# One block of a hybrid mLSTM decoder on Trainium2: the turned keys taken from the score products

## The chip, the cores and the metric

The kernel runs on one core of one Trainium2 chip. The metric is the device time of one execution in microseconds (us). The kernel before takes 1497.92 us, the median of three runs (1495.53 to 1499.62).

## What is computed

The program is one decoder block over 1024 positions of width 1024 in float32: a projection into 6664 columns, an mLSTM with 4 heads of 256 features beside a pooling branch, gates that merge the two, an output projection, and a gated feed-forward part. The change lies in the mLSTM. Cut to what matters, the reference computes for each head and each chunk of positions:

```
s = jnp.einsum('bhld,bhsd->bhls', qc, kc) * dexp          # scores, causal
num = w_inter[..., None] * jnp.einsum('bhvk,bhlk->bhlv', c_state, qc) + jnp.einsum('bhls,bhsv->bhlv', s, vc)
c_state = decay[..., None, None] * c_state + jnp.einsum('bhsv,bhsk->bhvk', vc * w[..., None], kc)
```

`dexp` is zero where the key's position `s` is later than the query's position `l`. The scores contract over the features of a key, the state over its positions, so the keys are needed in two orientations.

## The kernel before

Every float32 operand of a large product is split into two parts, a high part rounded to the engine's reduced float32 (`F32R`) and the rest (`split`, L131 and L132: a cast on ScalarE, a subtraction on VectorE). A product is then three matmuls, high by high, high by low and low by high (`mm3`, L143 to L145). The operands are written feature-major, 128 features on the partitions.

The mLSTM stage works on 16 items, 4 heads by 4 chunks of 256 positions (`items`, `c` is the chunk, `NC` is 4). For each item:

- `prepare` loads the keys `raw` (feature-major, two halves of 128 features), splits them into `k`, loads the two parts of the queries into `q`, the values into `v`, a row of gate numbers into `u`. Except in a head's last chunk it calls `turned`: four transposes on TensorE (L573, 128 by 128 each) put the keys position-major into one PSUM bank with the tag `aux`, and for each block of 128 positions ScalarE (L577) and VectorE (L578) scale them and split them into `kt`.
- `scores` makes the products of keys and queries, 12 matmuls of 256 columns into one bank: for both blocks `i` of 128 key positions and both feature halves `dk`, against all 256 query positions. Then it builds the decay factors in `dt`, multiplies them with the scores (L625) and splits the result into `ph` and `pl`. For the second block of keys only the second 128 query positions are read from the bank (`slice(384, 512)`).
- `update` makes the next state from `kt` and `v` (12 matmuls of 258 columns) and splits it into `cs`.
- `attend` makes the outputs from `cs` and `q`, from `v` and `ph`/`pl`, normalises them, turns them back (L683) and stores them into `ya`.

`second_branch` (L155, 24 matmuls of 512 columns a call) is put between the items as further work for TensorE; `project` makes its products. The loop runs over the items: it prepares item n+2, updates the state with item n, makes the scores of item n+1, then attends item n. The order in which each engine issues its instructions is not that of the code: a scheduler places them by its own forecast of times, and each engine then works in that order, waiting on semaphores. There are six PSUM banks with the tag `mm` and two with the tag `aux`; a bank is reused once all its readers are done.

Of the kernel before, what the change touches and what calls it, by code (L numbers as in the profile page):

```python
# [8 lines left out]
F32 = mybir.dt.float32  # L9
# [57 lines left out]
def tile_hybrid_block(ctx, tc, x, xt, consts, params, w_fm, w_v, w_pool, w_a, w_b, w_out, w_gate, w_up, w_down, out):  # L67
# [54 lines left out]
    def bank(tag="mm"):  # L122
        return psp.tile([P, 512], F32, tag=tag, name=tag, bufs=BANKS[tag])
# [429 lines left out]
    with ExitStack() as c4:  # L553
        t1 = pool(c4, "t1", 1)
        rc = pool(c4, "rc", 6)
        kp_ = pool(c4, "kp", 3)
        qp = pool(c4, "qp", 3)
        pp = pool(c4, "pp", 4)
        t2 = pool(c4, "t2", 2)
        vp = pool(c4, "vp", 3)  # L560
        ktp = pool(c4, "ktp", 3)

        def chunk(base, h, c):
            t = rc.tile([P, 2, 256], F32, tag="rc", name="rc")
            nc.sync.dma_start(out=t, in_=z_d[base + 2 * h:base + 2 * h + 2, :, c * 256:(c + 1) * 256].rearrange("i p n -> p i n"))
            return t

        def turned(dst, raw, scales):

            ps = bank("aux")  # L570
            for i in range(2):
                for f in range(2):
                    nc.tensor.transpose(out=ps[:, i * 256 + f * P:i * 256 + (f + 1) * P], in_=raw[:, f, i * P:(i + 1) * P], identity=ident)  # L573
            for i in range(2):
                src = ps[:, i * 256:(i + 1) * 256]
                hi, lo = dst[:, 0, i, 0:DH], dst[:, 1, i, 0:DH]
                nc.scalar.activation(out=hi, in_=src, func=AF.Copy, scale=scales[i])  # L577
                nc.vector.scalar_tensor_tensor(out=lo, in0=src, scalar=scales[i], in1=hi.bitcast(F32), op0=ALU.mult, op1=ALU.subtract)  # L578

        def prepare(h, c):  # L580
            it = {}
            raw = chunk(Z_K, h, c)
            k = it["k"] = kp_.tile([P, 2, 2, 256], F32R, tag="k", name="k")
            split(k[:, 0], k[:, 1], raw)
            it["made"] = split.last
            q = it["q"] = qp.tile([P, 2, 2, 256], F32R, tag="q", name="q")
            for a in range(2):
                src = q_d[a, 2 * h:2 * h + 2, :, c * 256:(c + 1) * 256]
                nc.sync.dma_start(out=q[:, a].bitcast(F32), in_=src.rearrange("i p n -> p i n"))
            u = it["u"] = t1.tile([P, 256], F32, tag="u", name="u", bufs=3)  # L590
            nc.sync.dma_start(out=u, in_=r_d[h, c * 256:(c + 1) * 256].partition_broadcast(P))
            v = it["v"] = vp.tile([P, 2, 2, VW], F32R, tag="v", name="v")
            nc.vector.tensor_copy(out=v[:, :, :, DH:VW], in_=norm[:, :, 2 * c:2 * c + 2, :])
            for a in range(2):
                src = v_d[a, c * 256:(c + 1) * 256, h * DH:(h + 1) * DH]
                it["loaded"] = nc.sync.dma_start(out=v[:, a, :, 0:DH].bitcast(F32), in_=src.rearrange("(i p) n -> p i n", p=P))
            if c < NC - 1:
                kt = it["kt"] = ktp.tile([P, 2, 2, DH], F32R, tag="kt", name="kt")
                turned(kt, raw, [e_put[:, 2 * c + i, h:h + 1] for i in range(2)])
            return it  # L600

        def scores(h, c, it):

            k, q, u = it["k"], it["q"], it["u"]
            ps = bank()
            for i in range(2):
                for dk in range(2):
                    l = [k[:, a, dk, i * P:(i + 1) * P] for a in range(2)]
                    r = [q[:, a, dk, :] for a in range(2)]
                    mm3(ps[:, i * 256:(i + 1) * 256], l, r, dk == 0, dk == 1)  # L610
            dt = t2.tile([P, 512], F32, tag="dt", name="dt")
            ph = pp.tile([P, 512], F32R, tag="p", name="ph")
            pl = pp.tile([P, 512], F32R, tag="p", name="pl")
            for i, jj in ((0, 0), (1, 1), (0, 1)):
                o = dt[:, i * 256 + jj * P:i * 256 + (jj + 1) * P]
                uu, b = u[:, jj * P:(jj + 1) * P], cd[:, jj - i, 2 * c + i, h:h + 1]
                if i < jj:
                    nc.scalar.activation(out=o, in_=uu, func=AF.Exp, bias=b, scale=-1.0)
                else:

                    nc.vector.tensor_scalar(out=o, in0=uu, scalar1=b, scalar2=0.0, op0=ALU.subtract, op1=ALU.max)
                    nc.scalar.activation(out=o, in_=o, func=AF.Exp, scale=-1.0)
                    nc.gpsimd.affine_select(out=o, in_=o, pattern=[[1, P]], compare_op=ALU.is_ge, fill=0.0, base=0, channel_multiplier=-1)
            for i, sl in enumerate((slice(0, 256), slice(384, 512))):
                nc.vector.scalar_tensor_tensor(out=dt[:, sl], in0=ps[:, sl], scalar=rsk[:, 2 * c + i:2 * c + i + 1], in1=dt[:, sl], op0=ALU.mult, op1=ALU.mult)  # L625
                split(ph[:, sl], pl[:, sl], dt[:, sl])
            it["p"] = ph, pl

# [16 lines left out]
        def attend(h, c, it, state):  # L645
            ss = t2.tile([P, 2], F32, tag="ss", name="ss")
            rd = t2.tile([P, 2], F32, tag="rd", name="rd")
            q, v, pr = it["q"], it["v"], it["p"]
            nums = []
            for jj in range(2):  # L650
                cl = 2 * c + jj
                num = t2.tile([P, VW], F32, tag="num", name="num", bufs=4)
                if c > 0:
                    ps = bank()
                    for dk in range(2):
                        mm3(ps[:, :VW], [q[:, a, dk, jj * P:(jj + 1) * P] for a in range(2)], [state[1][:, a, dk, :] for a in range(2)], dk == 0, dk == 1)
                    nc.scalar.activation(out=num, in_=ps[:, :VW], func=AF.Copy, scale=e_get[:, cl, h:h + 1])
                ps = bank()
                for i in range(jj + 1):
                    o = i * 256 + jj * P  # L660
                    mm3(ps[:, :VW], [a[:, o:o + P] for a in pr], [v[:, a, i, :] for a in range(2)], i == 0, i == jj)
                if c > 0:
                    nc.vector.tensor_add(out=num, in0=ps[:, :VW], in1=num)
                else:
                    nc.scalar.copy(out=num, in_=ps[:, :VW])
                r, den = rd[:, jj:jj + 1], num[:, DH:DH + 1]
                nc.vector.tensor_scalar(out=r, in0=den, scalar1=-1.0, scalar2=enm[:, cl, h:h + 1], op0=ALU.mult, op1=ALU.max)
                nc.vector.tensor_max(out=r, in0=den, in1=r)
                nc.vector.reciprocal(out=r, in_=r)

                nc.scalar.activation(out=rsb[:, jj * DH:(jj + 1) * DH], in_=num[:, :DH], func=AF.Square, scale=r, accum_out=ss[:, jj:jj + 1])
                nums.append(num)
            ms = t2.tile([P, 2], F32, tag="ms", name="ms")
            nc.vector.tensor_scalar(out=ms, in0=ss, scalar1=1.0 / DH, scalar2=EPS, op0=ALU.mult, op1=ALU.add)
            rs = t2.tile([P, 2], F32, tag="rs", name="rs")
            nc.gpsimd.tensor_tensor(out=rs, in0=ms, in1=nhalf[:, 0:2], op=ALU.pow)
            nc.vector.tensor_mul(out=rs, in0=rs, in1=rd)
            tr = bank("aux")
            for jj in range(2):
                hf = t2.tile([P, DH], F32, tag="hf", name="hf")  # L680
                nc.scalar.activation(out=hf, in_=nums[jj][:, :DH], func=AF.Copy, scale=rs[:, jj:jj + 1])
                for f in range(2):
                    nc.tensor.transpose(out=tr[:, f * 256 + jj * P:f * 256 + (jj + 1) * P], in_=hf[:, f * P:(f + 1) * P], identity=ident)  # L683
            sl = slice(c * 256, (c + 1) * 256)
            o = chunk(Z_O, h, c)
            for f in range(2):
                nc.vector.scalar_tensor_tensor(
                    out=o[:, f, :], in0=tr[:, f * 256:(f + 1) * 256], scalar=col(A_MH, 2 * h + f), in1=o[:, f, :], op0=ALU.mult, op1=ALU.mult)
            if h < H - 1:
                split(*(t[:, :, sl] for t in yat[h]), o)  # L690
                return
            for f in range(2):
                split(*(a[f][:, sl] for a in ya[h]), o[:, f, :])
# [33 lines left out]
        for n, (h, c) in enumerate(items):  # L727
            prepare_item(n + 2)
            if c == 0:
# [2 lines left out]
                    ya.append([[t[:, f, :] for f in range(2)] for t in yat[h]])  # L732
                else:
                    ya.append([[keep.tile([P, WIDE], F32R, tag="x", name="ya")[:, :S] for _ in range(2)] for _ in range(2)])
            nxt = update(h, c, its[n], state) if c < NC - 1 else None
            if n + 1 < len(items):
                scores(*items[n + 1], its[n + 1])
            attend(h, c, its[n], state)
            state = nxt
            for _ in range(YB[n]):  # L740
# [415 lines left out]
```

## Time and profile before

| | |
|---|---|
| median of three runs | 1497.92 us (1495.53 to 1499.62) |
| the profiled execution | 1498.39 us, its span 1496.7 us |
| TensorE (PE) busy | 1475.3 us, 99% of the span, 7067 matmuls |
| VectorE (DVE) busy | 1122.8 us, 75% |
| ScalarE (ACT) busy | 725.6 us, 48% |
| mean granted clock of TensorE | 0.996 of full speed |

A row of the profile gives the engine, the line of the kernel, the operation, and the names of what is written and read (`mm<-q,k` is a matmul into a bank `mm` with `q` moving and `k` as the weights). The duration of a matmul in such a row is the time from its start to its end, and matmuls overlap: a row of 392 ns says nothing of how close the next one follows. That is read from the starts in the timeline. PEld is the loading of weights, which overlaps the matmuls.

### The profile page before, as it was taken

How to read it: one execution, taken by the hardware profiler on the slowest of the kernel's cores; microseconds unless marked ns; L12 is line 12 of the kernel's file. 1: busy time of each engine (PE TensorE's matmuls, PEld its weight loads, DVE VectorE, ACT ScalarE, POOL GpSimd, SP SyncE). 2: the span in 40 equal slices, each digit the busy share in tenths (PEclk: the TensorE clock that was granted, in tenths of full speed). 3: DMA queues.
4: the chain of work that ended last, by engine and by line, in shares of the span. 5: the costliest groups of instructions: out<-in, count | busy, mean ns of one | idle time of the engine just before them, and what ended most of it. 6: DMA issues, size and time to landing. Idle time of an engine off the chain costs nothing.

```text
span 1496.7 us, 19610 instructions
## 1 busy us (share of the span) xinstructions
PE 1475.3 (99%) x7067; PEld 1245.3 (83%) x7067; DVE 1122.8 (75%) x2028; ACT 725.6 (48%) x1329; POOL 45.4 (3%) x74
## 2 busy tenths in 40 slices
PE   9999999999999999999999999999999999999997
PEld 9998888878887789997888778888888887888886
DVE  5757878797876678765557779888888885658945
ACT  6475655556553468772233455444444443332322
POOL 0000000000000011210000000000000000000022
PEclk9999999999999999999999999999999999999998
DMA  6662433243433498837534325443444435979653
GB/s 212 197 247 86 154 125 128 99 142 113 141 106 120 159 313 283 255 103 253 183 99 141 99 85 186 166 159 138 169 155 141 160 119 195 356 280 379 240 190 133
DMA packets 102448, 262.18 MB, mean 175 GB/s; under 512 B 9932, under 2 KB 47948, under 8 KB 102352
## 3 DMA queue, kind: packets, MB, share of 16 engines
q1 hardware_dynamic: 86608, 220.57, 42.6%
q10 hardware_dynamic: 15744, 40.38, 7.2%
q8 instruction: 55, 0.90, 0.2%
q14 instruction: 41, 0.34, 0.1%
HBM read 172.29 MB, written 88.62 MB: 174 GB/s over the span
## 4 chain that ended last, share of the span: by engine, by line
PE 94%; DMA 3%; DVE 2%; issue 1%; ACT 0%; SPq 0%; POOLq 0%; POOL 0%; DVEq 0%; ACTq 0%
PE mm L143 25%; PE mm L145 25%; PE mm L144 25%; PE mm L155 13%; PE aux L143 1%; PE aux L144 1%; PE aux L145 1%; DMA v<-v_d 1%; DMA tg<-tg_d 0%; DMA raw<-in_w_up 0%; PE mm L524 0%; DMA x<-in_xt 0%; PE aux L683 0%; DMA yb<-yb_d 0%; DMA rc<-z_d 0%
## 5 line engine op out<-in xcount | busy, mean ns | idle before, releaser
L131 ACT CAST s<-raw 128x512 fp32r<-128x512 f32 x220 | 133.6, 621 | 200.6 <-PE mm L145 164.1
L132 DVE TENSOR_TENSOR s<-raw,s 128x512 fp32r<-128x512 f32 x220 | 148.5, 687 | 30.1 <-ACT s L131 29.1
L143 PE MATMUL mm<-fd,s 128*128 128x512 f32 x352 | 137.7, 392 | 5.1 <-DVE e L234 2.7
L143 PE MATMUL mm<-zd,s 128*128 128x512 f32 x352 | 137.4, 393 | 0.3 <-DVE o L234 0.3
L144 PE MATMUL mm<-fd,s 128*128 128x512 f32 x352 | 137.7, 391 | 0.0
L145 PE MATMUL mm<-fd,s 128*128 128x512 f32 x352 | 137.5, 391 | 0.0
L145 PE MATMUL mm<-zd,s 128*128 128x512 f32 x352 | 137.3, 390 | 0.0
L144 PE MATMUL mm<-zd,s 128*128 128x512 f32 x352 | 137.1, 389 | 0.0
L143 PE MATMUL mm<-zb,s 128*128 128x512 f32 x264 | 103.9, 394 | 0.0
L144 PE MATMUL mm<-zb,s 128*128 128x512 f32 x264 | 102.8, 389 | 0.0
L145 PE MATMUL mm<-zb,s 128*128 128x512 f32 x264 | 102.7, 390 | 0.0
L144 PE MATMUL mm<-fb,s 128*128 128x512 f32 x264 | 102.7, 389 | 0.0
L143 PE MATMUL mm<-fb,s 128*128 128x512 f32 x264 | 102.7, 389 | 0.0
L145 PE MATMUL mm<-fb,s 128*128 128x512 f32 x264 | 102.7, 389 | 0.0
L144 PE MATMUL mm<-tg,a 128*128 128x512 f32 (+1 forms) x266 | 100.2, 377 | 0.0
L145 PE MATMUL mm<-tg,a 128*128 128x512 f32 (+1 forms) x266 | 100.0, 377 | 0.0
L143 PE MATMUL mm<-tg,a 128*128 128x512 f32 (+1 forms) x266 | 100.0, 377 | 0.0
L143 PEld LDWEIGHTS mm<-fd,s 128*128 128x128 f32 x352 | 66.4, 189 | 20.4 <-DVE e L234 3.2
L145 PEld LDWEIGHTS mm<-fd,s 128*128 128x128 f32 x352 | 66.5, 189 | 14.3 <-DVE s L132 0.4
L143 PEld LDWEIGHTS mm<-zd,s 128*128 128x128 f32 x352 | 66.1, 188 | 14.8 <-DVE o L234 0.8
L144 PEld LDWEIGHTS mm<-zd,s 128*128 128x128 f32 x352 | 66.1, 188 | 14.1 <-issue 0.5
L144 PEld LDWEIGHTS mm<-fd,s 128*128 128x128 f32 x352 | 66.4, 189 | 13.7
(345 smaller groups left out, 3508.5 us busy)
## 6 DMA issues: line engine op xcount, KB each, us to landing
tg_d<-t SPq DMA_DIRECT2D x77, 512.0 KB, 3.1
tg<-tg_d SPq DMA_DIRECT2D x77, 512.0 KB, 6.1
raw<-in_w_fm SPq DMA_DIRECT2D x44, 512.0 KB, 3.9
z_d<-o ACTq DMA_DIRECT2D x24, 512.0 KB, 2.9
raw<-in_w_gate SPq DMA_DIRECT2D x22, 512.0 KB, 3.7
raw<-in_w_up SPq DMA_DIRECT2D x22, 512.0 KB, 5.1
q_d<-x ACTq DMA_DIRECT2D x16, 512.0 KB, 2.7
rc<-z_d SPq DMA_DIRECT2D x32, 256.0 KB, 5.0
```

Source lines behind the costliest of these rows:

```text
L131: hi_made = cast(out=hi, in_=src)
L132: split.last = hi_made.ins, nc.vector.tensor_sub(out=lo, in0=src, in1=hi.bitcast(F32)).ins
L143: nc.tensor.matmul(out, lhsT=l[0], rhs=r[0], start=start, stop=False, skip_group_check=resume)
L144: nc.tensor.matmul(out, lhsT=l[0], rhs=r[1], start=False, stop=False, skip_group_check=resume)
L145: mm3.last = nc.tensor.matmul(out, lhsT=l[1], rhs=r[0], start=False, stop=stop, skip_group_check=resume)
L155: nc.tensor.matmul(ps[half], lhsT=l[a], rhs=r[half][b], start=(k == 0 and (a, b) == (0, 0)), stop=(k == nk - 1 and a == 1),)
```

## The change

`turned` no longer has transposes. Three standing tiles `q0`, `q1`, `q2` (printed below with the scheduler's numbers, as `q_4430`, `q_4431`, `q_4432`) take the place of the pool `q`: each holds the identity, the two feature halves of the queries' high part, the identity again, and the low part's halves. In `scores`, for all chunks but a head's last, the matmuls with high queries run over the queries and the identity beside them, so that the same weights give the scores and the keys turned, in one bank. For the first block of keys that makes, for each feature half, 384, 256 and 384 columns; for the second block, whose scores are now made for the second 128 query positions alone, 256, 128 and 256. The two blocks go to two banks, the first `mm`, the second `aux`. In a head's last chunk the second block's six matmuls shrink from 256 to 128 columns. `kt` has two buffers where it had three, and the loop makes the scores of item n+1 ahead of the update with item n.

```
-            ps = bank("aux")
-            for i in range(2):
-                for f in range(2):
-                    nc.tensor.transpose(out=ps[:, i * 256 + f * P:i * 256 + (f + 1) * P], in_=raw[:, f, i * P:(i + 1) * P], identity=ident)
...
-        ktp = pool(c4, "ktp", 3)
+        ktp = pool(c4, "ktp", 2)
...
+        qs = [t1.tile([P, 5 * 256], F32R, name=f"q{n}") for n in range(3)]
+        for t in qs:
+            for o in (0, 5 * P):
+                nc.vector.tensor_copy(out=t[:, o:o + P], in_=ident)
+
+        def blocks(t):
+            return t.rearrange("p (a n) -> p a n", n=P)
+
+        def turned(dst, src, scale):
+
+            hi, lo = (blocks(dst[:, a]) for a in range(2))
+            nc.scalar.activation(out=hi, in_=src, func=AF.Copy, scale=scale)
+            nc.vector.scalar_tensor_tensor(out=lo, in0=src, scalar=scale, in1=hi.bitcast(F32), op0=ALU.mult, op1=ALU.subtract)
...
-            q = it["q"] = qp.tile([P, 2, 2, 256], F32R, tag="q", name="q")
+            qt = it["qt"] = qs[len(its) % len(qs)]
+            q = it["q"] = [qt[:, o:o + 512].rearrange("p (i n) -> p i n", i=2) for o in (P, 6 * P)]
...
-            ps = bank()
-            for i in range(2):
-                for dk in range(2):
-                    l = [k[:, a, dk, i * P:(i + 1) * P] for a in range(2)]
-                    r = [q[:, a, dk, :] for a in range(2)]
-                    mm3(ps[:, i * 256:(i + 1) * 256], l, r, dk == 0, dk == 1)
+                s = []
+                for i in range(2):
+
+                    n = (2 - i) * P
+                    ps = bank("aux" if i else "mm")[:, :n + 2 * P]
+                    b = blocks(ps)
+                    for dk in range(2):
+                        l = [k[:, a, dk, i * P:(i + 1) * P] for a in range(2)]
+                        part = b[:, dk:dk + 3 - i]
+                        wide = blocks(it["qt"][:, dk * 3 * P:(dk + 1) * 3 * P])
+                        if i:
+                            wide = wide[:, 1:3] if dk else wide[:, 0:3:2]
+                        nc.tensor.matmul(part, lhsT=l[0], rhs=wide, start=dk == 0, stop=False, skip_group_check=True)
+                        nc.tensor.matmul(ps[:, P:P + n], lhsT=l[0], rhs=q[1][:, dk, i * P:], start=False, stop=False, skip_group_check=True)
+                        nc.tensor.matmul(part, lhsT=l[1], rhs=wide, start=False, stop=dk == 1, skip_group_check=True)
+                    turned(kt[:, :, i], b[:, 0::3 - i], e_put[:, 2 * c + i, h:h + 1])
+                    s.append(ps[:, P:P + n])
+            else:
+                ps = bank()
+                for i in range(2):
+                    for dk in range(2):
+                        l = [k[:, a, dk, i * P:(i + 1) * P] for a in range(2)]
+                        mm3(ps[:, i * 256 + i * P:(i + 1) * 256], l, [q[a][:, dk, i * P:] for a in range(2)], dk == 0, dk == 1)
+                s = [ps[:, 0:256], ps[:, 384:512]]
...
-                nc.vector.scalar_tensor_tensor(out=dt[:, sl], in0=ps[:, sl], scalar=rsk[:, 2 * c + i:2 * c + i + 1], in1=dt[:, sl], op0=ALU.mult, op1=ALU.mult)
+                nc.vector.scalar_tensor_tensor(out=dt[:, sl], in0=s[i], scalar=rsk[:, 2 * c + i:2 * c + i + 1], in1=dt[:, sl], op0=ALU.mult, op1=ALU.mult)
...
-            nxt = update(h, c, its[n], state) if c < NC - 1 else None
             if n + 1 < len(items):
                 scores(*items[n + 1], its[n + 1])
+            nxt = update(h, c, its[n], state) if c < NC - 1 else None
```

Three places of the order matter below. The first is TensorE's order where the projections (`zd`, `s`) end and the mLSTM stage begins. Before:

```order
L145 MATMUL mm<-zd_140,s 128x512
L573 MATMUL aux<-cst,rc 128x128 [waits DMAHW5_49,PE_49]
L573 MATMUL aux<-cst,rc 128x128 x3
L143 MATMUL mm<-q,k 128x256 [waits DMAHW6_49,Activation_49]
L155 MATMUL mm<-yb,wbh 128x512 x4
L155 MATMUL mm<-yb,wbl 128x512 [waits DVE_49]
```

And now:

```order
L145 MATMUL mm<-zd_140,s 128x512
L619 MATMUL mm<-q_4430,k 128x384 [waits DMAHW6_49,DVE_49,Activation_49]
L619 MATMUL aux<-q_4430,k 128x256 [waits PE_49]
L155 MATMUL mm<-yb,wbh 128x512 x4
L155 MATMUL mm<-yb,wbl 128x512 [waits DVE_49]
```

The four transposes are gone from ahead of the first call of `second_branch`, and two wide score matmuls stand where one of 256 columns stood; the wait for VectorE at `wbl` remains.

The second place is VectorE's order at the same time, where `wbl` is made. Before:

```order
L466 TENSOR_TENSOR o<-o,rsb 128x512 [waits DVE_49]
L593 COPY v<-norm 128x4x2 x2
L468 TENSOR_TENSOR o<-mm,rsb 128x512 [waits PE_49]
L593 COPY v<-norm 128x4x2
L132 TENSOR_TENSOR wbl<-raw,wbh 128x1024 [waits DMAHW1_49,Activation_49]
```

And now:

```order
L466 TENSOR_TENSOR o<-o,rsb 128x512 [waits DVE_49]
L571 CAST q_4430<-cst 128x128 x2
L571 CAST q_4431<-cst 128x128 x2
L571 CAST q_4432<-cst 128x128 x2
L596 COPY v<-norm 128x4x2
L596 COPY v<-norm 128x4x2 [waits PE_49]
L468 TENSOR_TENSOR o<-mm,rsb 128x512 [waits PE_49]
L596 COPY v<-norm 128x4x2
L132 TENSOR_TENSOR wbl<-raw,wbh 128x1024 [waits DMAHW1_49,Activation_49]
```

Six copies of the identity have come in ahead of `L468`, which waits for TensorE.

The third place is VectorE's order for the first two items. Before:

```order
L621 TENSOR_SCALAR dt<-u,cd 128x128
L578 SCALAR_TENSOR_TENSOR kt<-aux,e_put,kt 128x256 [waits Activation_49] x2
L132 TENSOR_TENSOR k<-rc,k 128x512 [waits DMAHW3_49,Activation_49]
L621 TENSOR_SCALAR dt<-u,cd 128x128 [waits DMAHW7_49]
L621 TENSOR_SCALAR dt<-u,cd 128x128
L625 SCALAR_TENSOR_TENSOR dt<-mm,rsk,dt 128x256 [waits PE_49,Pool_49]
L625 SCALAR_TENSOR_TENSOR dt<-mm,rsk,dt 128x128 [waits Pool_49]
```

And now:

```order
L132 TENSOR_TENSOR k<-rc,k 128x512 [waits DMAHW3_49,Activation_49]
L641 TENSOR_SCALAR dt<-u,cd 128x128 [waits DMAHW7_49]
L641 TENSOR_SCALAR dt<-u,cd 128x128
L580 SCALAR_TENSOR_TENSOR kt<-mm,e_put,kt 128x256 [waits Activation_49]
L645 SCALAR_TENSOR_TENSOR dt<-mm,rsk,dt 128x256 [waits Pool_49]
L580 SCALAR_TENSOR_TENSOR kt<-aux,e_put,kt 128x256 [waits Activation_49]
L645 SCALAR_TENSOR_TENSOR dt<-aux,rsk,dt 128x128 [waits Pool_49]
L580 SCALAR_TENSOR_TENSOR kt<-mm,e_put,kt 128x256 [waits Activation_49]
L645 SCALAR_TENSOR_TENSOR dt<-mm,rsk,dt 128x256 [waits Pool_49]
L132 TENSOR_TENSOR pl<-dt,ph 128x256 [waits Activation_49]
L580 SCALAR_TENSOR_TENSOR kt<-aux,e_put,kt 128x256 [waits Activation_49]
```

The making of the first item's `kt` has moved from ahead of its scores to behind them, among the scalings of the scores of the first and the second item.

## Rows read from the trace of the kernel before

**Rows 1.** The page: busy time of the engines, and the chain that ended last by engine.
```profile
PE 1475.3 (99%) x7067; PEld 1245.3 (83%) x7067; DVE 1122.8 (75%) x2028; ACT 725.6 (48%) x1329; POOL 45.4 (3%) x74
...
PE 94%; DMA 3%; DVE 2%; issue 1%; ACT 0%; SPq 0%; POOLq 0%; POOL 0%; DVEq 0%; ACTq 0%
```
**Rows 2.** Busy time by stretch; columns: us, PE, PEld, DVE, ACT, POOL, clock, DMA share, GB/s.
```profile
528.00:545.00 17.00, 16.15 (x101) 14.25 (x101) 12.65 (x30) 12.01 (x27) 1.08 (x4) 1.00 0.83 275
545.00:560.00 15.00, 15.00 (x106) 14.06 (x105) 12.50 (x46) 12.58 (x35) 3.06 (x8) 1.00 1.07 372
560.00:600.00 40.00, 40.00 (x290) 37.79 (x289) 34.74 (x127) 33.47 (x97) 6.21 (x14) 1.00 0.89 288
600.00:640.00 40.00, 39.94 (x263) 36.27 (x262) 29.29 (x106) 30.90 (x88) 8.41 (x16) 1.00 0.79 251
640.00:662.00 22.00, 22.00 (x176) 21.51 (x175) 18.39 (x61) 17.35 (x47) 2.70 (x5) 1.00 0.41 133
```
**Rows 3.** Timeline of PE, columns: start us, duration us, what; 512, 344 and 256 columns.
```profile
526.04 0.39 PE L143 MATMUL mm<-zd,s 128*128 128x512 f32 x1
...
526.95 0.39 PE L144 MATMUL mm<-zd,s 128*128 128x512 f32 x1
...
8.31 0.32 PE L144 MATMUL mm<-wv,zb 128*128 128x344 f32 x1
...
9.41 0.32 PE L145 MATMUL mm<-wv,zb 128*128 128x344 f32 x1
...
577.00 0.28 PE L144 MATMUL mm<-q,k 128*128 128x256 f32 x1
...
578.19 0.28 PE L145 MATMUL mm<-q,k 128*128 128x256 f32 x1
```
**Rows 4.** The chain that ended last, in order of time: four transposes of the keys.
```profile
545.11 0.44 PE aux L573 x4
```
**Rows 5.** Timeline of PE: products of one column, and plain float32 ones of 512 columns.
```profile
1463.33 1.62 PE L999 MATMUL aux<-cst,sq 128*128 128x1 f32 x14
1464.81 0.48 PE L143 MATMUL mm<-tg,a 128*128 128x512 f32 x1
...
507.05 1.88 PE L524 MATMUL mm<-x,raw 128*128 128x512 f32 x4
508.37 0.79 PE L143 MATMUL mm<-zb,s 128*128 128x512 f32 x1
```
**Rows 6.** The chain that ended last: four of those plain float32 matmul records.
```profile
507.21 1.72 PE mm L524 x4
```
**Rows 7.** Timeline of VectorE, and one row of PE, where the stage begins.
```profile
530.01 0.24 DVE L593 CAST v<-norm 128x8 fp32r<-128x8 f32 x2
531.41 0.69 DVE L468 TENSOR_TENSOR o<-mm,rsb 128x512 f32<-128x512 f32 x1 [1.16 <-PE mm L145]
...
532.09 2.35 DVE L132 TENSOR_TENSOR wbl<-raw,wbh 128x1024 fp32r<-128x1024 f32 x2
...
533.36 0.50 PE L155 MATMUL mm<-yb,wbl 128*128 128x512 f32 x1 [0.52 <-DVE wbl L132]
```
**Rows 8.** Groups by line and shape, 525 to 690 us: count, then busy us, mean ns.
```profile
L578 DVE SCALAR_TENSOR_TENSOR kt<-aux,e_put,kt 128x256 fp32r<-128x256 f32 x24 | 11.5, 477 | 1.1 <-ACT kt L577 1.0
L577 ACT ACTIVATE kt<-aux,e_put 128x256 fp32r<-128x256 f32 x24 | 11.3, 471 | 1.4 <-PE aux L573 1.3
...
L621 DVE TENSOR_SCALAR dt<-u,cd 128x128 f32<-128x128 f32 x32 | 7.8, 282 | 0.0
L625 DVE SCALAR_TENSOR_TENSOR dt<-mm,rsk,dt 128x256 f32<-128x256 f32 x16 | 7.7, 479 | 3.6 <-PE mm L145 3.6
```
**Rows 9.** Timeline of PE: its waits where the feed-forward part begins.
```profile
857.07 0.50 PE L143 MATMUL mm<-fd,s 128*128 128x512 f32 x1 [1.29 <-ACT s L131]
860.57 0.50 PE L143 MATMUL mm<-fd,s 128*128 128x512 f32 x1 [1.12 <-ACT e L230]
869.25 0.50 PE L143 MATMUL mm<-fd,s 128*128 128x512 f32 x1 [1.95 <-DVE e L234]
```

More of the change, by code (lines that the diff above doesn't have):

```diff
@@ L556, in tile_hybrid_block @@
         kp_ = pool(c4, "kp", 3)
-        qp = pool(c4, "qp", 3)
         pp = pool(c4, "pp", 4)
@@ L566, in chunk @@
             return t
-        def turned(dst, raw, scales):
-            ps = bank("aux")
-            for i in range(2):
-                for f in range(2):
-                    nc.tensor.transpose(out=ps[:, i * 256 + f * P:i * 256 + (f + 1) * P], in_=raw[:, f, i * P:(i + 1) * P], identity=ident)
-            for i in range(2):
[L575 to L578, printed above, removed]
+        qs = [t1.tile([P, 5 * 256], F32R, name=f"q{n}") for n in range(3)]
[8 more added lines that the diff above has]
+            nc.vector.scalar_tensor_tensor(out=lo, in0=src, scalar=scale, in1=hi.bitcast(F32), op0=ALU.mult, op1=ALU.subtract)
         def prepare(h, c):
@@ L585, in prepare @@
             it["made"] = split.last
-            q = it["q"] = qp.tile([P, 2, 2, 256], F32R, tag="q", name="q")
+            qt = it["qt"] = qs[len(its) % len(qs)]
+            q = it["q"] = [qt[:, o:o + 512].rearrange("p (i n) -> p i n", i=2) for o in (P, 6 * P)]
             for a in range(2):
                 src = q_d[a, 2 * h:2 * h + 2, :, c * 256:(c + 1) * 256]
-                nc.sync.dma_start(out=q[:, a].bitcast(F32), in_=src.rearrange("i p n -> p i n"))
+                nc.sync.dma_start(out=q[a].bitcast(F32), in_=src.rearrange("i p n -> p i n"))
             u = it["u"] = t1.tile([P, 256], F32, tag="u", name="u", bufs=3)
@@ L596, in prepare @@
                 it["loaded"] = nc.sync.dma_start(out=v[:, a, :, 0:DH].bitcast(F32), in_=src.rearrange("(i p) n -> p i n", p=P))
-            if c < NC - 1:
-                kt = it["kt"] = ktp.tile([P, 2, 2, DH], F32R, tag="kt", name="kt")
-                turned(kt, raw, [e_put[:, 2 * c + i, h:h + 1] for i in range(2)])
             return it
@@ L604, in scores @@
             k, q, u = it["k"], it["q"], it["u"]
-            ps = bank()
-            for i in range(2):
-                for dk in range(2):
-                    l = [k[:, a, dk, i * P:(i + 1) * P] for a in range(2)]
-                    r = [q[:, a, dk, :] for a in range(2)]
-                    mm3(ps[:, i * 256:(i + 1) * 256], l, r, dk == 0, dk == 1)
+            if c < NC - 1:
+                kt = it["kt"] = ktp.tile([P, 2, 2, DH], F32R, tag="kt", name="kt")
+                s = []
[21 more added lines that the diff above has]
+                s = [ps[:, 0:256], ps[:, 384:512]]
             dt = t2.tile([P, 512], F32, tag="dt", name="dt")
@@ L655, in attend @@
                     for dk in range(2):
-                        mm3(ps[:, :VW], [q[:, a, dk, jj * P:(jj + 1) * P] for a in range(2)], [state[1][:, a, dk, :] for a in range(2)], dk == 0, dk == 1)
+                        mm3(ps[:, :VW], [q[a][:, dk, jj * P:(jj + 1) * P] for a in range(2)], [state[1][:, a, dk, :] for a in range(2)], dk == 0, dk == 1)
                     nc.scalar.activation(out=num, in_=ps[:, :VW], func=AF.Copy, scale=e_get[:, cl, h:h + 1])
```

## The prediction

> **What bounds the kernel now.** I read the page first. TensorE is busy for 99% of the span, and 94% of the chain that ended last lies on it [rows 1]. That only says that it is never idle for long, so I looked at the stretch that the change touches. The mLSTM stage fills 528 to 662 us, and there TensorE is busy for 133.1 of 134 us at the full clock (1.00, which is the 2.4 GHz level); from 545 to 600 us it has no idle time at all [rows 2]. So time that is taken out of TensorE's queue in this stage comes off the end, unless another engine takes over. VectorE is the next candidate: 87% from 560 to 600 us, 84% from 640 to 662 us [rows 2]. The DMAs are as good as full from 545 to 560 us (1.07) and at 0.89 behind that, yet TensorE does not wait for them.
>
> The durations that profile rows give for matmuls cannot be added up, since matmuls overlap. The price of one is the distance to the next start. For 512 columns that is 0.91 us over 4 steps, 0.227 us; for 344 columns 1.10 over 7, 0.157; for 256 columns 1.19 over 10, 0.119, which I round to 0.120 [rows 3]. These three lie on a line of 0.42 ns a column with 13 ns on top. On that line 384 columns cost 0.174 us, between the 344 and the 512 of the rows, so I trust it. Four transposes of 128 columns take 0.44 us of the chain, 0.11 each [rows 4].
>
> **The change part by part.** Transposes: 12 items have them (4 heads by 3 chunks), 12 x 0.44 = 5.3 us removed.
>
> Scores of these 12 items: before, 12 matmuls of 256 columns, 12 x 0.120 = 1.44 us. Now 4 of 384, 6 of 256 and 2 of 128: 4 x 0.174 + 6 x 0.120 = 1.416 us and two times x, where x is the price of a 128-column matmul with operands in reduced float32.
>
> Scores of the 4 last chunks: before 1.44 us; now 6 of 256 and 6 of 128: 0.72 us and six times x.
>
> So x is wanted 48 times, and no row of the kernel before has such a matmul. The bounds: from below the line through [rows 3], 128 x 0.42 + 13 = 67 ns. From above the rate of plain float32: its product of 512 columns leaves two records in the trace (the code has 8 such products in L524, the trace 16 records), four records take 1.72 us [rows 6], so a product takes 0.86 us and 128 columns of it 0.215. The nearest rows lie between. The transposes stream 128 columns and take 110 ns, not 67 [rows 4]. Products of a single column, which stream next to nothing, take 1.48 us for 14 records, 106 ns each [rows 5], whereas four plain records of 512 columns take 430 ns each [rows 5, 6]. Something that does not shrink with the columns holds 128-column weights at 106 to 110 ns, and I take that to be the loading of the weights, which each matmul has. I take x = 0.110.
>
> With it an item with transposes goes from 1.44 + 0.44 = 1.88 to 1.416 + 0.22 = 1.636 us, 0.244 saved, times 12 is 2.93 us. A last chunk goes from 1.44 to 0.72 + 0.66 = 1.38, 0.06 saved, times 4 is 0.24. Together **3.17 us**. With x = 0.067 it is 12 x 0.33 + 4 x 0.318 = 5.2 us; with x = 0.215 it is 12 x 0.034 - 4 x 0.57 = 1.9 us lost.
>
> The Trainium skill has another price: TensorE: Matmul & The Clock Gate, section Back-to-back issue gap, gives a sustained spacing of some 81 ns for 128 columns; by it the sum would be an estimated 12 x 0.302 + 4 x 0.234 = 4.6 us. The trace does not agree at other sizes: the page's 131 ns for 512 columns stand against 227 here.
>
> First item: its matmuls ahead of `second_branch` shrink from 0.44 + 0.12 to 0.174 + 0.120 us, but right behind them TensorE waits 0.52 us for VectorE's `wbl` [rows 7]. These 0.27 us become a longer wait and are lost.
>
> Identity copies: six copies on VectorE, once. The nearest rows are 0.12 us (half of 0.24 for two small casts) and 0.28 (an operation of 128 x 128) [rows 7, 8], so 0.7 to 1.7 us. They stand ahead of `L468`, before which VectorE is idle for 1.16 us waiting for TensorE [rows 7]. That idle time hides them; what is over, 0 to 0.5 us, would delay `wbl` and with it TensorE. I take nothing. The identity's blocks are never written again, and the query loads are as many, on the same queue, with a tile to reuse after three items as before.
>
> Turned keys, later: the two operations per block that make `kt` stay, 0.47 us on ScalarE and 0.48 on VectorE [rows 8], but they follow the scores instead of running one or two items ahead. In the loop scores are made an item ahead of their update. In TensorE's new order some thirty matmuls stand between the last score product of an item and the first that needs what it made; at the tightest place, a head's second item, it is ten, about 1.1 us against the 0.47 of ScalarE's high part, with the low part wanted later still. I cost this at nothing. At the first two items there is no such lead. VectorE has eight instructions from the first `kt` to the last of the second item, at up to 0.48 us each 3.8 us, while TensorE's cover is the second item's scores (1.64 us) and the first update (12 x 0.120 = 1.44). A wait of 0 to 1.2 us (with ScalarE's 0.47 ahead), I take 0.6. Banks: the first block's scores are held longer by the two makings of `kt`, a microsecond in a ring of six; nothing. The second block's take the turn in `aux` that the transposes had; nothing.
>
> The rest of the program: orders shift by a few instructions where the feed-forward part begins, where TensorE waits 1.29, 1.12 and 1.95 us [rows 9]. These waits may grow or shrink; I cost it at nothing, with 1 us to either side.
>
> **Sum:** 3.17 - 0.27 - 0.6 = 2.3 us. Against the profiled execution's own 1498.39 us that makes 1496.1; that execution stands 0.47 us above the median of the runs shown, so as a median I forecast 1497.92 - 2.3 = **1495.6 us**, 0.15% less. About 0.3% (4.5 us) is what a measurement of this kernel can tell from no change: under 1493.4 counts as faster, over 1502.4 as slower.
>
> **The rivals.** *Narrow matmuls at the line's price.* If weights of reduced float32 load faster than the plain ones of [rows 4, 5], x is 0.067 and the gain 5.2 - 0.87 = 4.3 us: 1493.6. For it: the 256-column matmuls show no sign of a floor, they lie on the line [rows 3]. Against it: both rows of 128-column weights under narrow streams. The skill's 81 ns lead an estimated 3.7 us down the same way.
>
> *Narrow matmuls at the plain rate.* If operands in reduced float32 keep their speed only at the widths seen here, 256 and more [rows 3], x is 0.215: 1.9 + 0.87 = 2.7 us lost, 1500.7. Then the change doesn't do what it says: halving the columns makes them dearer.
>
> *Turned keys become a wait.* TensorE works in order, so if it comes to the update before VectorE has made `kt`, all behind it stands still. From the last score matmul to the last part of `kt` it takes 0.47 + 0.48 us, and 0.48 more for each operation ahead of it on VectorE [rows 8], which is 87% busy at its worst [rows 2]. It decides from a mean wait of 0.24 us per item on: that eats the gain of an item. At 0.6 us on 11 items it is 2.3 - 6.6 = 4.3 us lost: 1502.2. Against it: the order's distances of ten to thirty matmuls, 1.1 to 3.5 us.
>
> *VectorE bounds the stage.* If its 87% are in truth a chain without slack, TensorE only waits more: 1497.9. Against it: no wait of TensorE in 55 us.
>
> **How the numbers follow.** Forecast 0.48, line price 0.21, plain rate 0.12, waits for the keys 0.12, VectorE 0.07. The forecast's own range is 1493.5 to 1498. Half of the line price's chance and a tenth of the forecast's lie under 1493.4: faster 0.16. Half of the waits and a third of the plain rate lie over 1502.4, since the run itself spreads by 2 us: slower 0.10. The rest, 0.74, is no change that can be told. The range reaches from the line price less the runs' lower spread (1493.6 - 2) to the plain rate: 1491.6 to 1500.9.
>
> **What would show it.** TensorE's starts behind a 128-column score matmul at about 110 ns, behind a 384-column one at 174; the mLSTM stage shorter by 2 to 3 us, with TensorE's idle time in it longer by less than 1 us, most of it at `wbl` and at the first `kt`. Steps of 67 or 215 ns, or waits of the update on `kt` in every item, would make me wrong.

## The result and the profile after

The changed kernel takes 1505.26 us, the median of 6 runs (1502.39 to 1507.89); the kernel before took 1498.74 in the same comparison (1495.53 to 1499.62). The ratio is 1.0045 (95% interval 1.0034 to 1.0056): **slower by 0.45%**, where 0.15% faster was forecast, and outside the range. The profiled execution took 1505.55 us, its span is 1503.7, 7.0 us longer than before.

The page of the changed kernel, to be laid beside [rows 1]:

```profile
PE 1477.6 (98%) x7019; PEld 1244.4 (83%) x7019; DVE 1126.3 (75%) x2034; ACT 729.0 (48%) x1329; POOL 46.5 (3%) x74
...
PE 91%; DVE 4%; DMA 2%; ACT 1%; issue 1%; SPq 0%; POOL 0%; POOLq 0%; DVEq 0%; ACTq 0%
```

The 48 transposes are gone, and the chain that ended last has lost 3 points on TensorE (PE) to VectorE (DVE) and ScalarE (ACT). The table by stretch shows where (columns as in [rows 2]):

```profile
560.00:600.00 40.00, 36.30 (x230) 33.01 (x231) 32.46 (x113) 32.12 (x88) 7.65 (x14) 0.96 0.84 270
600.00:640.00 40.00, 38.56 (x256) 35.31 (x257) 30.94 (x110) 30.50 (x86) 7.60 (x15) 1.00 0.77 243
...
662.00:670.00 8.00, 6.12 (x43) 5.13 (x42) 6.38 (x22) 5.83 (x17) 0.70 (x1) 1.00 0.00 0
```

From 560 to 600 us TensorE was busy all the time before [rows 2]; now it idles for 3.7 us, and part of that stretch ran at a lower clock (0.96 in the mean). The stage ends at 669 us, not at 662.

To say what a wait costs I priced TensorE's queue: every matmul gets the step of its width (0.227 us for 512 columns, 0.174 for 384, 0.120 for 256 and 258, 0.110 for 128), and what the starts lie further apart than that is **lost time**. The measure is taken from the first matmul of the second call of `second_branch` to that of the eighth, most of the stage. Before, this stretch takes 87.65 us: 86.97 of work, 0.68 lost. Now it takes 94.68 us: 85.08 of work and 9.60 lost (1.50 of it is the lower clock). So 1.89 us of work went, and 8.92 us of lost time came. Of the 7.04 us on the whole span, 7.03 arise here; 2.4 more arise behind the eighth call, and small shifts of both signs outside the stage take as much back.

The timeline of TensorE in the changed kernel (start us, duration us, what, and in brackets the idle time and who ended it):

```profile
531.71 0.50 PE L155 MATMUL mm<-yb,wbl 128*128 128x512 f32 x1 [0.77 <-DVE wbl L132]
...
555.28 0.27 PE L145 MATMUL mm<-q,k 128*128 128x128 f32 x1
555.39 0.28 PE L143 MATMUL mm<-q,k 128*128 128x128 f32 x1
555.50 0.28 PE L144 MATMUL mm<-q,k 128*128 128x128 f32 x1
...
562.08 0.39 PE L145 MATMUL mm<-v,pl 128*128 128x258 f32 x1 [1.20 <-DVE pl L132]
...
573.20 0.38 PE L703 MATMUL aux<-cst,hf 128*128 128x128 f32 x2
573.34 0.37 PE L619 MATMUL aux<-q,k 128*128 128x256 f32 x1
573.54 0.22 PE L620 MATMUL aux<-q,k 128*128 128x128 f32 x1
573.60 0.33 PE L621 MATMUL aux<-q,k 128*128 128x256 f32 x1
573.77 0.28 PE L619 MATMUL aux<-q,k 128*128 128x256 f32 x1
...
591.13 0.34 PE L143 MATMUL mm<-v,kt 128*128 128x258 f32 x1
...
592.04 0.36 PE L619 MATMUL aux<-q,k 128*128 128x256 f32 x1
...
595.53 0.29 PE L144 MATMUL mm<-v,kt 128*128 128x258 f32 x1
...
597.03 0.41 PE L145 MATMUL mm<-v,kt 128*128 128x258 f32 x2
...
599.83 0.39 PE L143 MATMUL mm<-cs,q 128*128 128x258 f32 x1 [1.57 <-ACT cs L131]
...
633.52 0.39 PE L143 MATMUL mm<-cs,q 128*128 128x258 f32 x1 [1.25 <-ACT cs L131]
```

What is to be seen, from the top. A run of 128-column products steps at 0.11 us, as forecast. The second block's products (L619 to L621 into `aux`) stand right behind the turned outputs (`hf`, L703) of an earlier item: 573.20 and 573.34. The first block of that item had ended at 563 us. The twelve items with turned keys are counted from 0 here: in eight of the items 2 to 11 the second block starts 4.9 to 13.1 us behind the last wide product of the first, in the other two 1.0 and 1.8 us.

Then one case through. At 591.13 us the update of an item begins with its first block of turned keys, yet the second block's products, which make the other half of these keys, come only at 592.04. ScalarE and VectorE turn to them when they can:

```profile
593.45 0.47 ACT L579 ACTIVATE kt<-aux,e_put 128x256 fp32r<-128x256 f32 x1
...
599.16 0.62 ACT L131 CAST cs<-c 128x516 fp32r<-128x516 f32 x1 [0.18 <-DVE c L660]
```

```profile
594.37 0.48 DVE L580 SCALAR_TENSOR_TENSOR kt<-aux,e_put,kt 128x256 fp32r<-128x256 f32 x1
...
598.26 0.87 DVE L660 SCALAR_TENSOR_TENSOR c<-c,e_keep,mm 128x258 f32<-128x258 f32 x2
```

The high part is ready at 593.92, the low part at 594.85. TensorE has the products with them at 595.17 to 595.53 and 597.03, so the making of the state `c` begins at 598.26, that of its high part `cs` at 599.16, and TensorE waits 1.57 us for `cs`. The profile names `cs`, not `kt`: **the keys were late, and the lateness showed two steps further down.** An update is 12 matmuls, 1.3 us from first to last start when they stand together; here it is spread over 6.0 us. Over the 12 updates the median spread was 1.6 us before and is 2.6 now.

The rows of ScalarE's groups (530 to 668 us; count, busy us, mean ns, idle time before and who ended it) show it waiting for the second block at the making of `kt`:

```profile
L579 ACT ACTIVATE kt<-aux,e_put 128x256 fp32r<-128x256 f32 x12 | 5.7, 477 | 2.8 <-PE aux L621 2.7
```

The first block's keys, made from `mm`, are ready (high part) a median of 5.8 us ahead of their update's first product; the second block's, made from `aux`, 0.07 us. Before, the later half was ready a median of 3.4 us ahead. It came after the update's first product in two of the twelve updates, by 1.9 us at most; now the second block's does so in five, by up to 5.6. I call that the **lead of the keys**.

### The profile page after: what moved, and what is told of

Read it like the earlier page. It is cut to its first block, busy times and chain, and to the rows that moved or that the text cites. A ratio compares the mean times of both kernels' runs of the same rounds, so it can differ in the third digit from the quotient of the medians.

```text
span 1503.7 us, 19506 instructions
## 1 busy us (share of the span) xinstructions
PE 1477.6 (98%) x7019; PEld 1244.4 (83%) x7019; DVE 1126.3 (75%) x2034; ACT 729.0 (48%) x1329; POOL 46.5 (3%) x74
## 4 chain that ended last, share of the span: by engine, by line
PE 91%; DVE 4%; DMA 2%; ACT 1%; issue 1%; SPq 0%; POOL 0%; POOLq 0%; DVEq 0%; ACTq 0%
PE mm L143 25%; PE mm L145 24%; PE mm L144 24%; PE mm L155 13%; PE aux L143 1%; PE aux L145 1%; PE aux L144 1%; DMA tg<-tg_d 1%; DMA raw<-in_w_up 0%; PE mm L524 0%; DMA yb<-yb_d 0%; DMA u<-r_d 0%; ACT rsb L691 0%; PE aux L703 0%; DVE rc L707 0%
## 5 line engine op out<-in xcount | busy, mean ns | idle before, releaser
L143 PEld LDWEIGHTS mm<-zd,s 128*128 128x128 f32 x352 | 66.1, 188 | 14.7 <-DVE o L234 0.8
```

Of the source, the lines that this page charges most:

```text
L143: nc.tensor.matmul(out, lhsT=l[0], rhs=r[0], start=start, stop=False, skip_group_check=resume)
```

## The experiments

The theories: **B**, the second block's place in `aux` is what costs; **K**, the turned keys are late; **L**, the swap in the loop (scores of item n+1 ahead of the update with item n) costs by itself. The runs soon showed that B and K are cause and effect, with L an addition of its own.

### The swap undone alone

```
+            nxt = update(h, c, its[n], state) if c < NC - 1 else None
             if n + 1 < len(items):
                 scores(*items[n + 1], its[n + 1])
-            nxt = update(h, c, its[n], state) if c < NC - 1 else None
```

> The changed kernel with the loop put back: the update with item n ahead of the scores of item n+1. Theory K (keys late: the making of kt now follows the scores and sits in VectorE's and ScalarE's queues where it is wanted at once) and theory B (banks: the second block's scores wait for one of two aux banks): little changes, 1503 to 1507 us, waits in the mLSTM stage still 9 us or more above those of before. Theory L (the loop order alone: the state has one block of scores less between its update and its use): the waits for cs go and the time comes to 1496 to 1498.

Measured: 1511.75 us, ratio 1.0079 (1.0066 to 1.0093), above what any of the theories asked for. 9.54 us lost in the stretch, as many as in the changed kernel; the second block's keys now come 1.8 us after the update's first product (median). The swap alone was not the cause; with late keys it even helps the whole. Where the 6.5 us beyond the changed kernel arise isn't shown: the profiled execution, 1507.61 us, was the fastest of the five.

### The second block in `mm`

```
-                    ps = bank("aux" if i else "mm")[:, :n + 2 * P]
+                    ps = bank("mm")[:, :n + 2 * P]
```

> The changed kernel with the second block's scores in a bank with the tag mm in place of aux. Theory B: the second block's six matmuls stand right behind the first block's in TensorE's order, the waits shrink from 13 us to under 5, and the time comes to 1496 to 1499. Theories K and L: 1503 to 1507, as the changed kernel.

Measured: 1499.45 us, ratio 1.0005 (0.9996 to 1.0014). One expression of the kernel gives 5.8 us back, 0.45 us more than theory B's range allows. The same 85.08 us of work in the stretch, 3.28 lost; lead of the keys 5.7 us, spread of an update 1.3. From 560 to 600 us TensorE is busy again; the largest wait that is left in the stretch is on another operand:

```profile
560.00:600.00 40.00, 39.63 (x268) 36.19 (x267) 34.32 (x118) 34.14 (x94) 7.02 (x14) 1.00 0.90 296
```

```profile
616.73 0.50 PE L155 MATMUL mm<-yb,wbh 128*128 128x512 f32 x1 [0.81 <-ACT num L677]
```

### The halved scores alone, on the kernel before

```
-                    r = [q[:, a, dk, :] for a in range(2)]
-                    mm3(ps[:, i * 256:(i + 1) * 256], l, r, dk == 0, dk == 1)
+                    r = [q[:, a, dk, i * P:] for a in range(2)]
+                    mm3(ps[:, i * 256 + i * P:(i + 1) * 256], l, r, dk == 0, dk == 1)
```

> The kernel before with one part of the change alone: scores of the second block for the second 128 query positions only, transposes kept. All theories: if a 128-column matmul costs 0.110 us, 16 items save 6 x 0.01 us, 1 us in all, 1497 to 1499; at 0.067 us it would be 5 us less, 1493 to 1494; at 0.215 us 9 us more.

Measured: 1501.85 us, ratio 1.0019 (1.0010 to 1.0028). By the steps, TensorE's work in the whole stage fell by 0.96 us (16 items of six products at 0.110 for 0.120), yet the kernel is 3.4 us slower: one wait of 1.33 us has come into the stretch, and the lower clock at the start of the feed-forward part lasts 6.8 us where it lasted 3.4. So less work in the queue, with other starts, can cost a few us by itself. That is the size of what no count of work foresees in this kernel.

### The swap alone, on the kernel before

The edit of the first experiment the other way round.

> The kernel before with one part of the change alone: scores of item n+1 ahead of the update with item n. Theory L: the waits for cs at the heads' starts appear here too, 3 us or more, 1501 to 1505. Theories K and B: within 1.5 us of before, 1497 to 1500.

Measured: 1504.67 us, ratio 1.0038 (1.0025 to 1.0050). 5.02 us lost in the stretch, with keys that keep their lead (3.0 us). The biggest of its waits:

```profile
611.41 0.68 PE L683 MATMUL aux<-cst,hf 128*128 128x128 f32 x4 [1.41 <-DVE rc L687]
```

So the swap has a cost of its own where the keys are early. Theory L had asked for 3 us or more of waits on `cs`; there are 1.36 us of these in the stretch.

### Both undone

The edits of the first two experiments together.

> The kernel after with both earlier edits: the second block's scores in a bank mm, and the update of item n ahead of the scores of item n+1 as in the kernel before. Before is taken as 1498.5 us. Theory B (the bank in aux) with the swap as a second, separate cost, as the swap alone added 6 us to the kernel before: without both the full gain of 3 us comes out, about 1495.5, and TensorE idles under 3 us in the stage. Rival (the turned keys come late, and the swap is what gives them their lead): TensorE waits for kt or cs at the updates, 1502 or more, as the same undoing of the swap raised the kernel after from 1505 to 1511. Rival (any other order of the issue is as good as any other, by chance): anywhere from 1497 to 1503, without a wait on kt.

Measured: 1499.53 us, ratio 1.0000 (0.9991 to 1.0009). The time says that nothing was won, the trace says otherwise: the stretch takes 85.81 us, 1.84 less than before, with 0.73 lost. With these four kernels there is a table of two by two, lost time in the stretch in us:

| | second block in `aux` | in `mm` |
|---|---|---|
| scores ahead of the update | 9.60 | 3.28 |
| update first | 9.54 | 0.73 |

The 9.60 hold 1.50 us of the lower clock, the other three none. The bank costs 6.3 and 8.8 us, the swap 2.6 us, and that only with the bank in `mm`. `kt` has two buffers in all four, and with 0.73 us lost in the last, they are not what costs. The stage's gain is there; part of it is given back behind the stage, where the third weights of the next part come late. TensorE's timeline there, in this version:

```profile
689.72 0.73 PE L155 MATMUL mm<-ya,wal 128*128 128x512 f32 x2 [1.93 <-DVE wal L132]
```

Before, no wait stood at `wal`; one of 1.15 us stood at `wah`. Behind these 1.93 us the clock is at its lower level for 3.4 us. This profile is of the slowest of the 11 executions, 1501.89 us.

### Three banks of `aux`

```
-BANKS = {"mm": 6, "aux": 2}
+BANKS = {"mm": 5, "aux": 3}
```

> The kernel after with three banks of the tag aux and five of mm. Theory B in its narrow form (the second block and the turned outputs take turns in only two banks): the third bank lets the second block follow its first block, TensorE's idle time in the stage falls from 12.8 us to 7 or less, 1499 to 1501 us. Rival (eight banks are too few once the scores take two for each item, whatever their tag): the fifth bank of mm is missed as much as the third of aux helps, 1504 to 1508.

Measured: 1519.14 us, ratio 1.0150 (1.0130 to 1.0171), beyond both theories. 17.45 us lost in the stretch (2.95 at the lower clock). The second block still stands 8.5 to 13.8 us behind its first in seven of the items 2 to 11, as in the changed kernel, and the lead of its keys is 0.6 us. A third bank doesn't bring the second block forward, and the time is worse; that the missing bank of `mm` makes it so is likely, but no run shows it apart.

### Late keys alone, on the kernel before

```
-                turned(kt, raw, [e_put[:, 2 * c + i, h:h + 1] for i in range(2)])
...
+                turned(kt, it["raw"], [e_put[:, 2 * c + i, h:h + 1] for i in range(2)])
```

The removed line stood in `prepare`, the added one stands in `scores`, behind the products.

> The kernel before with its four transposes and the making of kt moved from the preparing of an item to behind its score products, nothing else. Theory K (keys that are made an item later become a wait): TensorE waits on kt at the updates, 1501 to 1505. Theory B (late keys cost nothing, the bank does): 1498.5 within 1.5 us, and less than 2 us of idle time in the stage.

Measured: 1514.52 us, ratio 1.0101 (1.0088 to 1.0115). 13.60 us lost in the stretch (3.00 at the lower clock); the lead of the keys is -1.6 us, an update is spread over 4.5 us. TensorE's waits now carry the name of the cause, 6.21 us of them in the stretch:

```profile
557.25 0.39 PE L143 MATMUL mm<-v,kt 128*128 128x258 f32 x1 [1.96 <-ACT kt L577]
```

Same matmuls, banks and columns as before: turning the keys late, by itself, costs 15.5 us, more than theory K asked for. The step that I had costed at nothing can cost several times what the whole change was to gain.

### The second block in `aux` alone, with early keys, on the kernel before

```
-            ps = bank("aux")
+            ps = bank("mm")
...
+            s = []
             for i in range(2):
+                ps = bank("aux" if i else "mm")
```

The first pair is the bank of the transposes, the second that of the scores.

> The kernel before with the second block's scores in a bank of their own with the tag aux (256 columns as before), and the transposes of the keys in a bank mm in exchange; columns, matmuls and the loop as before. Theory B (the score products in aux come behind the turned outputs): the second block falls behind its first by several us in TensorE's order, idle time in the stage of 5 us or more, 1502 to 1505. Rival (the bank costs only together with the swap of the loop or with the keys): 1498.5 within 1.5 us.

Measured: 1503.57 us, ratio 1.0029 (1.0017 to 1.0040), the 1502 to 1505 that theory B asked for, but not for its reason. The second block falls behind its first here too, by 5.5 to 15.7 us in twelve of the 16 items, and yet the stretch has 1.52 us lost, 0.84 more than before. Most of the rest is one wait where the stage begins, with 3.4 us of the lower clock behind it:

```profile
534.58 0.58 PE L145 MATMUL mm<-q,k 128*128 128x256 f32 x1 [2.81 <-DVE k L132]
```

With keys turned ahead of the scores (lead 11.3 us) the place of the second block in `aux` costs next to nothing in the loop. So the bank costs through the keys.

### The turned outputs out of `aux`

```
-            tr = bank("aux")
+            tr = bank("mm")
```

> The kernel after with the bank of the turned outputs (hf) taken from mm, so that the second block's scores have the two banks of aux to themselves. Before is taken as 1499 us. Theory T (the second block falls behind because it takes turns with the turned outputs): TensorE's order no longer has it 8 to 12 us behind its first block, the waits on pl, cs and kt go, 1498 to 1501. Rival (two tags part the two blocks whichever runs ahead: now the first blocks wait for one of six mm banks that the outputs take too, and their half of the keys is late): idle time of 8 us or more in the stage, 1503 to 1507.

Measured: 1612.50 us, ratio 1.0760 (1.0746 to 1.0774). Neither theory asked for 107 us. The order of the two blocks has turned round: for the items 4 to 11 the second block now starts 21 to 27 us ahead of the last wide product of its first, and TensorE, coming to it early, waits for the queries themselves:

```profile
579.62 0.38 PE L619 MATMUL aux<-q,k 128*128 128x256 f32 x1 [3.70 <-DMA q<-q_d]
```

33.1 us of waits in the stretch are on such loads, 14.7 on `hf`, and 69 of the stretch's 165 us ran at the lower clock. The time tells nothing on the theory; the order does: what held the second block back was its turn behind the outputs in `aux`.

### The second block's keys early, its scores in `aux`

```
+                for f in range(2):
+                    nc.tensor.transpose(out=ps[:, f * P:(f + 1) * P], in_=raw[:, f, P:2 * P], identity=ident)
+                turned(it["kt"][1], blocks(ps), e_put[:, 2 * c + 1, h:h + 1])
...
+                    if i:
+                        ps = bank("aux")[:, :P]
```

> The kernel after in which the second block's keys alone are turned by two transposes while the item is prepared (in a bank mm); its scores stay in aux, with 128 columns, and their order stays behind the turned outputs. TensorE has 12 x (6 x 0.110 + 2 x 0.110 - 0.70) = 2.2 us more to do than in the kernel after. Theory KB (the bank in aux costs because the second block's keys lose their lead): 1505.3 less some 9 us of waits plus 2.2, about 1498 to 1500. Rival (it costs because the second block's weighted scores, ph and pl, come late): the waits stay, 1505 to 1508.

Measured: 1507.60 us, ratio 1.0060 (1.0048 to 1.0072): by the time the theory failed. By the trace most of it stands. The second block still starts 6.5 to 15.7 us behind its first in nine of the items 2 to 11, yet the lost time in the stretch fell from 9.60 to 4.37 us, the updates stand together again (1.3 us), and no wait on `cs` of over 0.3 us is left. The same loop with the second block in `mm` lost 3.28, so early keys alone bring 5.2 of the bank's 6.3 us back. What ate the gain are the two one-off waits of the two versions above, at the stage's start and at `wal`, each with the lower clock behind it:

```profile
534.43 0.44 PE L634 MATMUL mm<-q,k 128*128 128x384 f32 x1 [3.04 <-DVE k L132]
...
698.10 0.50 PE L155 MATMUL mm<-ya,wal 128*128 128x512 f32 x1 [1.96 <-DVE wal L132]
```

Of the 4.37 us that are left 1.6 are waits on `num`; whether late `ph` and `pl` stand behind them was not taken apart.

### The version that follows

Second block in `mm`, update first, and behind the stage VectorE's third `wal` issued ahead of the gating of the second column, which is the order that the kernel before has there by itself. The code now also asks for each column's weights one turn of that loop ahead:

```
+            nxt = parts(wp, "w", load(w_a[j + 1]), "wa")
+            made = split.last[1]
...
+            with (tc.issue_after(made) if j == 1 else ExitStack()):
+                gated_a = nc.vector.tensor_mul(out=t, in0=ps[half], in1=t)
```

> The version with the second block in mm and the update first, and in the part behind the stage VectorE's low part of the third weights wa issued ahead of the gating of the second column of outputs, as in the kernel before, where in that version TensorE waited 1.93 us for it and fell to the lower clock for 3.4 us behind that. Theory (the stage has its gain, the wait behind it takes it back): 1499.5 less 1.9 to 3.4 us, 1496 to 1497.6. Rival (the wait only moves to the next weights): 1499 to 1500.

Measured: 1495.31 us (7 runs, 1490.93 to 1497.50) against 1498.45, ratio 0.9973 (0.9960 to 0.9986): **faster than both kernels.** Its page, and its timeline of TensorE (an update that stands together, and the wait at `wal`):

```profile
PE 1474.3 (99%) x7019; PEld 1243.9 (83%) x7019; DVE 1123.2 (75%) x2034; ACT 725.8 (49%) x1329; POOL 44.1 (3%) x74
```

```profile
588.76 0.28 PE L143 MATMUL mm<-v,kt 128*128 128x258 f32 x1
...
590.08 0.28 PE L145 MATMUL mm<-v,kt 128*128 128x258 f32 x1
...
688.32 0.50 PE L155 MATMUL mm<-ya,wal 128*128 128x512 f32 x1 [0.72 <-DVE wal L132]
```

The stretch takes 85.80 us, 0.72 lost. The wait at `wal` went from 1.93 to 0.72 us, and the lower clock behind it is gone. The two profiled executions, each the slowest of its runs, are 4.4 us apart: 3.2 us of lost time went between 685 and 700 us, where `wal` is, and 1.5 at the start of the feed-forward part, which the edit doesn't touch. How much of the 4.2 us between the medians the order at `wal` makes is so not shown beyond these 3.2.

## Why the prediction was wrong

**TensorE's work: right.** x was put at 0.110 us and measures 0.110 (two steps from 555.28 to 555.50 us). Between wider products a 128-column one lets its follower start early, and the next start pays: 0.06 us behind L620 and 0.17 behind L621 (573.54 to 573.77), 0.230 for the pair, as 0.110 and 0.120 make. The sum for the stage was 3.17 us; in the three versions with the second block in `mm` the whole stage's work, by the steps, fell from 129.34 to 126.18 us, 3.16. That only counts matmuls; that the prices hold shows in the version with both undone, whose stretch is 1.84 us shorter as measured, 1.89 by the count. The 81 ns that the Trainium skill gives for 128 columns (TensorE: Matmul & The Clock Gate, Back-to-back issue gap) don't agree with the trace's 110.

**First item: right.** 0.27 us were to turn into a longer wait at `wbl`; it went from 0.52 [rows 7] to 0.77.

**Identity copies: right.** 0.90 us on VectorE, in the idle time ahead of `L468`, which shrank from 1.16 to 0.38 us; `wbl` was not delayed.

**First keys: too dear, harmlessly.** 0.6 us were put down, none came in the changed kernel, 0.49 in the best version.

**The step that failed** is "The second block's take the turn in `aux` that the transposes had; nothing", with the one ahead of it, "I cost this at nothing", on the turned keys. The turn in `aux` was harmless for transposes of keys that had been loaded items ahead: the turns came early enough for a median lead of 3.4 us. Given to the scores it stands behind the turned outputs of an earlier item, and with it stand the scores, which make the keys. I had counted "some thirty matmuls" of lead from a score product to the update that needs it; in the order as it ran, 16 to 92 stand between an item's first block and its update, but never more than 24 behind the second block, and in four of the twelve updates the first product stands ahead of it. What was measured is 5.8 us of lead for the block in `mm` and 0.07 us for the block in `aux`. I read the order at the places where the first block stands, and did not look up the second block, the one on a ring of two. Of the 8.9 us of lost time that came, 6.3 go with the bank alone and 2.6 more with the swap, for which the prediction has no term. Together they made a forecast gain of 2.3 us into a loss of 6.5.

**The rivals.** "Turned keys become a wait" was the one that came true, at 0.12, and at 1502.2 it was too cheap by 3 us. The stated range ended at 1500.9 and so left out this rival, which the prediction itself had priced. Its test, waits of TensorE on `kt`, would have missed it: in the whole stage these are 0.08, 0.35 and 0.67 us. The kernel's order already reckons with late keys by setting their products back, so the loss appears at `cs` and `pl`. VectorE as a bound is refuted: from 560 to 600 us it is busy for 34.57 us in the best version, more than in the changed kernel (32.46), and TensorE waits less. Narrow matmuls at the line's price or at the plain rate are refuted by the measured step.

**The feed-forward start** was put at nothing within 1 us. The waits there are 1.15, 0.24 and 1.20 us for 1.29, 1.12 and 1.95 [rows 9], but the clock stays low for 6.8 us instead of 3.4; in lost time at the lower clock that is 2.90 for 1.53. The two nearly cancel.

## What to carry to other kernels

When an operation takes over another's buffer, don't compare how often the buffer turns, but what stands ahead in that turn and how long the new user can wait for it; then measure the lead, from when a value is made to when its first reader starts, for each ring apart. A wait that the trace names is the last link: spread-out groups of matmuls that used to stand together point to the operand that was late. And where a change takes work from the engine that bounds, look for its gain stage by stage, since one wait behind the stage can hide the whole of it.

## What was not expected of the hardware

The clock can fall behind waits that are short, and need not. In the changed kernel TensorE waited 0.22, 1.20 and 0.30 us between 560.0 and 563.5 us. From 563.9 to 567.3 us the granted clock was 0.50, the 1.2 GHz level, which cost 1.50 us on top of the 1.7 us of waits. The version with the swap alone undone comes to the same place with waits of 0.68, 0.70 and 0.42 us, and its clock stayed at 1.00, the 2.4 GHz level. First the changed kernel, then that version (columns as in [rows 2]):

```profile
560.00:563.90 3.90, 2.21 (x12) 1.68 (x13) 3.90 (x15) 2.90 (x9) 0.08 (x1) 1.00 1.05 396
563.90:567.30 3.40, 3.40 (x15) 3.11 (x14) 3.40 (x14) 2.12 (x7) 1.99 (x4) 0.50 1.09 349
```

```profile
560.00:563.90 3.90, 2.11 (x12) 1.58 (x12) 3.90 (x14) 2.91 (x9) 0.00 (x0) 1.00 1.05 396
563.90:567.30 3.40, 3.40 (x21) 3.03 (x21) 3.40 (x14) 2.12 (x8) 1.89 (x4) 1.00 1.09 349
```

The changed kernel's longer waits of 1.57 and 1.25 us (599.83, 633.52) were followed by no fall either, nor was the one of 0.81 us in the version with `mm` alone (616.73). So a wait can cost nearly twice what its row shows, and the waits' lengths alone don't tell which one will.
